# Opening of a two-layer encoder trunk: interleaved first products, token-order squares, and small matmuls at both ends

## The chip, the cores and the metric

The kernel runs on one core of one Trainium2 chip. Time is device microseconds of that core for one execution; the figure compared is the median of the runs of a kernel.

## The reference

One inference step of an encoder for two request groups, one prompt of 512 frames and eight running streams of 16 frames, 640 token columns together, each of 1024 channels, in float32. There are two layers. Each layer computes

- `x += 1/2 * SwiGLU(RMSNorm(x) * g1)` with 2816 hidden columns,
- a mixer: one projection of the norm, a short causal convolution, attention in a band of 64-frame chunks, two gates and an output product,
- a second half step of SwiGLU.

A final RMSNorm ends it. The part that matters here is the very first step and the very last one:

```python
def _rmsnorm(x, g):
    xf = x.astype(jnp.float32)
    y = xf * lax.rsqrt(jnp.mean(xf * xf, axis=-1, keepdims=True) + EPS)
    return y.astype(x.dtype) * g

def _swiglu(h, w_gu, w_down):
    gu = h @ w_gu
    g, u = jnp.split(gu, 2, axis=-1)
    return (jax.nn.silu(g) * u) @ w_down
```

## The kernel before

**Layout.** Channels lie on partitions: x is eight tiles `x[k]` of 128 channels by 640 tokens (SEQ + streams). [...] Weights come as a stream `wst` of slabs of 128 by 1024 (512 KB), each eight blocks of 128 by 128, through three buffers named `raw` (`load`, L245).

**Precision.** Every float32 product is made of three matmuls in a faster float32 format: each operand is split in a high part and a low part (what the high part leaves), and high x high, high x low and low x high are added up in PSUM (`multiply`, L372). So each slab is split too: ScalarE casts it to `whi` (L305), VectorE subtracts to get `wlo` (L310). `prep(i)` casts slab i and leaves its subtraction pending, `flush()` issues what is pending, `source(i)` loads a slab (and for later slabs adds pieces of it), `quiet()` takes the next prepared slab without preparing another. Three buffers each of `whi` and `wlo` exist.

**Seven products.** Most of the feed-forward layers use a scheme in which a 2 by 2 block product takes seven products instead of eight; its seven operands per pair of rows of x are `ex.ops[kp]`, tiles of 7 by 320 columns (high and low). They are made by `Expand.final` from the even row (`E`, three pieces) and the odd row (`O`, five pieces) of a pair.

**The opening** (`opening`, L606 on) does the first four gate and up columns of the first feed-forward layer as eight plain products of 8 rows x 3 x 2 = 48 matmuls, while the operands of the scheme are made beside them for what follows. The norm's factor `rho` is not known at the start, so the products are made of `x * g` alone, and `rho` is multiplied in afterwards. In the kernel before, product 0 follows the rows of x as they come in, then product 1; then ScalarE squares the eight rows of x (L571, L574), VectorE adds them up (L249), PE sums over partitions with a column of ones (`npsa`, L472), ScalarE takes the root (L585), VectorE the reciprocal and a diagonal (L589, L482), and PE spreads it over partitions with `ones` (`nbca`, L595) in row 1 of product 3. The operands of the scheme are made between products 2 and 6 by `final` (L521 to L556). A product writes `po`, one of two double-bank buffers of PSUM; `out(i)` takes it away, and product i + 2 needs that buffer.

**The order of work.** In this stage the orders of PE, VectorE and ScalarE are those in which the code is written (`manual_schedule`); each engine does its list strictly in that order and waits where an input is not there. From the sixth hidden column on only PE's order is written and a planner orders VectorE and ScalarE. Loads of x, weights and tokens are issued by SyncE's queue (SP), in order. In the opening the rows of x and quarters of slab 0 are issued alternately (L415, L421), with slabs 1 and up behind them.

**The end** (`Final.all`): the last down product is made in two parts of columns, 384 and 256 (`PARTS`). After each row of the second part its squares go into `npsf` by matmuls with a column of ones (L1939); then come a root (L1944), reciprocal, diagonal, and one matmul `nbcf` that spreads the result (L1954), and VectorE scales the eight rows and sends them out (L1958, L1960).

Of the kernel before, what the change touches and what calls it, by code (L numbers as in the profile page):

```python
# [10 lines left out]
F32 = mybir.dt.float32  # L11
# [5 lines left out]
P = 128  # L17
# [160 lines left out]


@with_exitstack  # L180
def trunk(ctx: ExitStack, tc: tile.TileContext, xin, wst, small, pbias, samplebias, kcache, vcache,
          yout, ko, vo, co):
    nc = tc.nc
    PE, DVE, ACT, POOL, SP = nc.tensor, nc.vector, nc.scalar, nc.gpsimd, nc.sync
# [123 lines left out]
    def flush():  # L308
        for lo, src, hi in pending:
            DVE.tensor_tensor(out=lo, in0=src, in1=hi.bitcast(F32), op=ALU.subtract)  # L310
        pending.clear()
# [102 lines left out]
    for k in range(KT):  # L414
        SP.dma_start(x[k], xin[:, k, :])  # L415

        if k == 0:
            raws.append(wp.tile([P, CH], F32, tag="raw", name="raw0", bufs=3))
        if k % 2 == 0:
            c = slice(k * P, (k + 2) * P)  # L420
            SP.dma_start(raws[0][:, c], wst[0][:, c])  # L421

    def norm(pool, name, goff, ssum):

# [64 lines left out]
    class Expand(Stats):  # L489
# [10 lines left out]
            self.sq = self.rest = None  # L500
            self.known = False

        def final(self, m, square=True):

            kp, odd = divmod(m, 2)
            n = f"{self.name}_{kp}"
            if not odd:

                self.E = self.fp.tile([P, 3, HT], F32, name=f"xe{n}", tag="even", bufs=1)
                hi = self.fp.tile([P, 7, HT], F32R, name=f"xhi{n}", tag=f"xhi{kp}")  # L510
                lo = self.fp.tile([P, 7, HT], F32R, name=f"xlo{n}", tag=f"xlo{kp}")
                self.ops.append((hi, lo))
            else:

                O = self.fp.tile([P, 5, HT], F32, name=f"xo{n}", tag="odd", bufs=1)
            E = self.E
            hi, lo = self.ops[kp]
            end = m == KT - 1
            g = sm[:, self.goff + m : self.goff + m + 1]
            B = O[:, 3:5] if odd else E[:, 0:3:2]  # L520
            ACT.activation(B, halves(x[m]), AF.Copy, scale=g)  # L521
            if square and end:
                self.sq = tmp(f"sq{self.name}_{m}")
            elif square:
                self.square(m)
            if not odd:
                DVE.tensor_tensor(out=E[:, 1], in0=E[:, 0], in1=E[:, 2], op=ALU.subtract)
                self.flush()
                ACT.copy(hi[:, 5:7], E[:, 0:2])
                self.late.append((lo[:, 5:7], E[:, 0:2], hi[:, 5:7]))  # L530
            else:
                self.flush()
                ACT.copy(hi[:, 3:5], O[:, 3:5])
# [3 lines left out]
                DVE.tensor_tensor(out=O[:, XT7], in0=O[:, 4], in1=E[:, 2], op=ALU.subtract)  # L537
                self.late.append((lo[:, 3:5], O[:, 3:5], hi[:, 3:5]))
                self.flush()

                def rest():
                    ACT.copy(hi[:, 0:3], O[:, 0:3])
# [5 lines left out]
                if not end:  # L548
# [53 lines left out]
    def opening(fp, name, goff, n, put, tails):  # L602

        ACT.copy(early, epst)  # L606
        ex = Expand(fp, name, goff)
        h = []
        whi, wlo = (wp.tile([P, CH], F32R, tag=f"w{t}", name=f"w{t}0", bufs=3) for t in ("hi", "lo"))
        ready.append((whi, wlo))  # L610
        for k in range(KT):
            g = sm[:, goff + k : goff + k + 1]
            hi = hp.tile([P, T], F32R, tag="hhi", name=f"hhi{name}_{k}")
            lo = hp.tile([P, T], F32R, tag="hlo", name=f"hlo{name}_{k}")
            ACT.activation(hi, x[k], AF.Copy, scale=g)
            c = slice(k * P, (k + 2) * P)
            if k % 2 == 0:
                ACT.copy(whi[:, c], raws[0][:, c])
            DVE.scalar_tensor_tensor(out=lo, in0=x[k], scalar=g, in1=hi.bitcast(F32),
                                     op0=ALU.mult, op1=ALU.subtract)  # L620
            if k % 2 == 0:
                DVE.tensor_tensor(out=wlo[:, c], in0=raws[0][:, c], in1=whi[:, c].bitcast(F32),
                                  op=ALU.subtract)
            h.append((hi, lo))
        flush()

        made = {2: (0, 1), 3: (2, 3), 4: (4,), 5: (5, 6), 6: (7,)}
        us, gs, ps = [], [], []

        def out(i):  # L630

            j, up = divmod(i, 2)
            if not up:
                gs.append(tmp(f"g{name}_{j}"))
                if j:
                    scaled(gs[j], ps[i], ex.rho)
                    ACT.activation(gs[j], gs[j], AF.Silu)
                else:
                    ACT.copy(halves(gs[j]), two(ps[i]))
# [9 lines left out]
        def begun():  # L649
            ex.total(att(f"nps{name}"))  # L650
            ex.root()
            ex.diagonal()

        at = {2: {4: begun}, 3: {1: lambda: ex.spread([att(f"nbc{name}_{a}")[:, :HT] for a in range(2)])}}
        for i in range(2 * n):
            ps.append(acc(f"po{name}_{i}"))
            product(ps[i], h, at.get(i, {}))
            if i > 1:
                out(i - 1)
            if i == 0:  # L660
                for k in range(KT):
                    ex.square(k)
                    ex.add()
                    if k == 1:
                        out(0)
                    if k == 4:
                        flush()
            if i == 1:
                continue
            if i == 3:  # L670
                g, u = gs[0], us[0]
                DVE.tensor_tensor(out=g, in0=g, in1=ex.rho, op=ALU.mult)
                ACT.activation(g, g, AF.Silu)
                DVE.tensor_tensor(out=u, in0=u, in1=ex.rho, op=ALU.mult)
            flush()
            for m in made.get(i, ()):
                ex.final(m, False)
            if i == 3:
                DVE.tensor_tensor(out=u, in0=u, in1=g, op=ALU.mult)
            if i == max(made):  # L680
                ex.rest()
        ahead()
        begin()
        out(2 * n - 1)

        def parts(j, u):
            hi = hp.tile([P, T], F32R, tag="hhi", name=f"ahi{name}_{j}")
            lo = hp.tile([P, T], F32R, tag="hlo", name=f"alo{name}_{j}")
            split(hi, lo, u)
            put(j, (hi, lo))  # L690


        for j in sorted(range(n), key=lambda j: j < 2):
            tails.append(lambda j=j: parts(j, us[j]))
        ex.rest = None
        return ex
# [1171 lines left out]
    class Final:  # L1868
# [8 lines left out]
        def all(self, ops):  # L1877
# [9 lines left out]
            for m in range(KT):  # L1887
# [173 lines left out]
def _layout(inputs):  # L2061
# [21 lines left out]
    return {"xin": xin, "wst": _stream(i), "small": small, "pbias": pbias, "samplebias": sbias, "kcache": kc, "vcache": vc}  # L2083


_OUTS = {
# [39 lines left out]
```

## Time and profile before

| | us |
|---|---|
| median of 3 runs | 2496.21 (2496.2 to 2496.61) |
| the profiled execution | 2496.66 |
| its span, first to last instruction | 2494.7 |
| PE busy / weight loads busy | 2478.1 / 2419.0 |
| VectorE busy | 2119.2 |
| ScalarE busy | 1450.0 |
| mean granted clock of TensorE | 0.998 |

In the profile, PE is TensorE's matmuls, PEld its weight loads, DVE VectorE, ACT ScalarE, POOL GpSimd, SP SyncE; L with a number is a line of the kernel; `out<-in` names the tile written and those read. A row in order of time has the start, the busy time, the instruction, how many were merged (x2), and in brackets the idle time before it with what ended it. Matmuls overlap, so the distance between starts tells more than the busy time. A float32 matmul that is not split appears as two passes, each with a weight load of its own.

### The profile page before, as it was taken

The page shows a single profiled execution, that of the slowest core. Times are in us where ns is not written, and L with a number is a line of the kernel's source. Part 1 is how long each engine was busy: PE and PEld are TensorE (multiplying, and loading weights), DVE is VectorE, ACT ScalarE, POOL GpSimd, SP SyncE. Part 2 cuts the span into 40 slices and gives each one's busy share as a digit, 9 for nine tenths or more (in the row PEclk, how much of TensorE's full clock was granted, in tenths as well). Part 3 has the DMA queues.
Part 4 walks back from the last instruction along what each step waited for, and adds up shares of the span by engine and source line. Part 5 has one row for each costly group of instructions (what it writes and reads, how often), then busy time and mean ns, then how long its engine had stood idle before and what let it go on. Part 6 is the DMA issues. An engine that isn't in the chain of part 4 may idle for free.

```text
span 2494.7 us, 43515 instructions
## 1 busy us (share of the span) xinstructions
PE 2478.1 (99%) x17048; PEld 2419.0 (97%) x17048; DVE 2119.2 (85%) x3322; ACT 1450.0 (58%) x2343; POOL 370.7 (15%) x445
## 2 busy tenths in 40 slices
PE   9999999999999999999999999999999999999998
PEld 8999999888999999999999999998899999999998
DVE  7888888878888899888798889888788888989887
ACT  7455556674666555555565555556646665555554
POOL 0011211211111011111001111221111110111111
PEclk9999999999999999999999999999999999999999
DMA  4245665335345344655435555643344553455554
GB/s 146 82 107 124 138 135 130 106 115 167 99 119 145 101 116 118 138 135 135 117 90 126 129 134 123 138 119 115 125 153 104 126 141 95 119 133 122 129 135 110
DMA packets 133261, 308.10 MB, mean 124 GB/s; under 512 B 12768, under 2 KB 76128, under 8 KB 133056
## 3 DMA queue, kind: packets, MB, share of 16 engines
q1 hardware_dynamic: 68976, 219.18, 27.3%
q0 software_dynamic: 63360, 85.50, 20.6%
q8 instruction: 133, 2.18, 0.4%
q10 hardware_dynamic: 720, 0.65, 0.1%
q14 instruction: 72, 0.59, 0.1%
HBM read 221.13 MB, written 7.94 MB: 92 GB/s over the span
## 4 chain that ended last, share of the span: by engine, by line
PE 94%; DVE 3%; ACT 2%; DMA 1%; issue 0%; SPq 0%; DVEq 0%; ACTq 0%
PE pab L395 12%; PE paa L395 11%; PE pcb L395 6%; PE pca L395 6%; PE daa L962 5%; PE dab L962 5%; PE po L372 4%; PE qa L395 4%; PE pbb L395 3%; PE pba L395 3%; PE dca L962 3%; PE dcb L962 3%; PE pda L372 2%; PE pv L1622 2%; PE ma_cv L395 2%; PE qc L395 2%
## 5 line engine op out<-in xcount | busy, mean ns | idle before, releaser
L310 DVE TENSOR_TENSOR wlo<-raw,whi 128x512 fp32r<-128x512 f32 (+1 forms) x583 | 598.6, 1030 | 236.1 <-ACT whi L305 230.6
L305 ACT CAST whi<-raw 128x512 fp32r<-128x512 f32 (+1 forms) x583 | 519.9, 897 | 348.0 <-PE pbb L395 44.6
L305 ACT CAST whi<-s 128x1024 fp32r<-128x1024 f32 (+1 forms) x164 | 153.6, 937 | 248.1 <-issue 107.8
L395 PE MATMUL pab<-xhib,whi 128*128 128x320 f32 x704 | 218.3, 310 | 0.4 <-DVE gb L249 0.4
L395 PE MATMUL pab<-xhib,wlo 128*128 128x320 f32 x704 | 217.4, 309 | 0.0
L395 PE MATMUL pab<-xlob,whi 128*128 128x320 f32 x704 | 217.4, 309 | 0.0
L395 PE MATMUL paa<-xhia,whi 128*128 128x320 f32 x640 | 198.0, 309 | 0.2 <-DVE ga L249 0.2
L395 PE MATMUL paa<-xloa,whi 128*128 128x320 f32 x640 | 197.6, 309 | 0.0
L395 PE MATMUL paa<-xhia,wlo 128*128 128x320 f32 x640 | 197.6, 309 | 0.0
L310 DVE TENSOR_TENSOR wlo<-s,whi 128x1024 fp32r<-128x1024 f32 (+1 forms) x164 | 176.6, 1077 | 10.4 <-ACT whi L305 10.4
L395 PEld LDWEIGHTS pab<-xhib,whi 128*128 128x128 f32 x704 | 132.2, 188 | 1.1 <-DVE gb L249 0.9
L395 PEld LDWEIGHTS pab<-xlob,whi 128*128 128x128 f32 x704 | 132.2, 188 | 0.2
L395 PEld LDWEIGHTS pab<-xhib,wlo 128*128 128x128 f32 x704 | 132.2, 188 | 0.0
L395 PEld LDWEIGHTS paa<-xhia,whi 128*128 128x128 f32 x640 | 120.2, 188 | 0.5 <-DVE ga L249 0.5
L395 PEld LDWEIGHTS paa<-xloa,whi 128*128 128x128 f32 x640 | 120.2, 188 | 0.1
L395 PEld LDWEIGHTS paa<-xhia,wlo 128*128 128x128 f32 x640 | 120.2, 188 | 0.0
L249 DVE TENSOR_TENSOR raw<-raw,raw 128x512 f32<-128x512 f32 x164 | 112.2, 684 | 1.8 <-DMA raw<-in_wst 0.2
L249 DVE TENSOR_TENSOR raw<-s,raw 128x512 f32<-128x512 f32 x164 | 112.3, 685 | 0.0
L395 PE MATMUL pcb<-xhib,whi 128*128 128x320 f32 x352 | 108.7, 309 | 0.0
L395 PE MATMUL pcb<-xlob,whi 128*128 128x320 f32 x352 | 108.7, 309 | 0.0
L395 PE MATMUL pcb<-xhib,wlo 128*128 128x320 f32 x352 | 108.7, 309 | 0.0
L986 POOL DMA_DIRECT2D x<-c_b x52 | 62.6, 1203 | 309.5 <-ACT c_b L979 134.5
(816 smaller groups left out, 8170.8 us busy)
## 6 DMA issues: line engine op xcount, KB each, us to landing
raw<-in_wst SPq DMA_DIRECT2D x375, 512.0 KB, 3.7
x<-c_b POOLq DMA_DIRECT2D x52, 320.0 KB, 5.1
x<-c_a POOLq DMA_DIRECT2D x50, 320.0 KB, 5.0
kc<-in_kcache SPq DMA_DIRECT2D x32, 256.0 KB, 4.1
vc<-in_vcache SPq DMA_DIRECT2D x16, 512.0 KB, 4.5
ub<-cbb POOLq DMA_DIRECT2D x42, 160.0 KB, 5.9
ua<-cba POOLq DMA_DIRECT2D x38, 160.0 KB, 5.4
x<-u_a POOLq DMA_DIRECT2D x18, 320.0 KB, 5.1
```

Source lines behind the costliest of these rows:

```text
L249: DVE.tensor_tensor(out=out, in0=a, in1=b, op=ALU.add)
L305: ACT.copy(hi[:, d], src[:, c])
L310: DVE.tensor_tensor(out=lo, in0=src, in1=hi.bitcast(F32), op=ALU.subtract)
L372: PE.matmul(ps[a] if isinstance(ps, list) else ps[:, a, :HT], w, x[:, a * HT : (a + 1) * HT], start=first and j == 0, stop=last and j == 2)
L395: PE.matmul(ps, a, b, start=start and kp == 0 and j == 0, stop=stop and kp == NP - 1 and j == 2, skip_group_check=True)
L962: PE.matmul(ps[u], w, y, start=start and i == 0 and j == 0, stop=i == 1 and j == 2, skip_group_check=True)
L986: POOL.dma_start(rows(r, cols), z, accum_op=ALU.add)
L1622: PE.matmul(pv[t], xx[:, t * P : (t + 1) * P], w[:, kk * AW : (kk + 1) * AW], start=c == 0 and kk == 0 and j == 0, stop=c == KT // 2 - 1 a ...
```

## The change

1. **Rows interleaved.** Products 0 and 1 run together: each row of x is multiplied into both before the next row (the last two rows together). For that, slab 1 is loaded and split in quarters like slab 0, alternating with the rows of x. For row 0, VectorE instead of ScalarE makes the two high weight parts.
2. **Odd rows kept.** The split of an odd row of x is written into its place among the operands of the scheme (pieces 3 and 4 of `ex.ops`), so that it is not made again. `Expand.final` is no longer called here; its steps are written out as `scale`, `mix`, `high`, `low`.
3. **Token squares.** The input has a second copy of x in token order (`xtok`, five tiles of 128 tokens by 1024 channels). It is loaded by nine transfers behind slab 2 and squared and summed along its rows, tokens 0, 2 and 4 on VectorE, 1 and 3 on ScalarE (all but the first in two halves). The ten npsa passes and the eight squares of rows with their seven additions go.
4. **Orders written out.** What ScalarE and VectorE do between the products is one written list, with the casts of slabs, the copies of products and the operands of the scheme in fixed places. The spread stands at row 3 of product 3 instead of row 1.
5. **Small matmuls.** `stir` issues matmuls of ones with ones that nothing reads: 15 at the start of the opening, 3 and 5 near the end, around the last sum of squares.

```diff
+    def stir(ps, n):
+        for _ in range(n):
+            PE.matmul(ps[:, :P], ones, ones, start=True, stop=True)
...
         if k == 0:
-            raws.append(wp.tile([P, CH], F32, tag="raw", name="raw0", bufs=3))
+            for n in range(2):
+                raws.append(wp.tile([P, CH], F32, tag="raw", name=f"raw{n}", bufs=3))
         if k % 2 == 0:
             c = slice(k * P, (k + 2) * P)
-            SP.dma_start(raws[0][:, c], wst[0][:, c])
+            for n in range(2):
+                SP.dma_start(raws[n][:, c], wst[n][:, c])
...
         ACT.copy(early, epst)
+        stir(att(f"stir{name}"), 15)
         ex = Expand(fp, name, goff)
+        ex.ps = fp.tile([P, NT], F32, name=f"sums{name}", bufs=1)
+        load(2)
+        z = fp.tile([P, D], F32, tag="s65", name=f"tok{name}_0", bufs=1)
+        toks = [[(z, ex.ps[:, 0:1])]]
+        rest = fp.tile([P, NT], F32, name=f"rest{name}", bufs=1)[:, 1:]
+        SP.dma_start(z, xtok[0])
+        for c in range(1, NT):
+            toks.append([])
+            for a, (tag, z) in enumerate((("hhi", ex.ps[:, c : c + 1]), ("hlo", rest[:, c - 1 : c]))):
+                t = hp.tile([P, T], F32, tag=tag, name=f"tok{name}_{c}{a}")[:, : D // 2]
+                toks[c].append((t, z))
+                SP.dma_start(t, xtok[c][:, a * D // 2 : (a + 1) * D // 2])
...
+            if odd:
+                hi, lo = (z[:, 3:5].rearrange("p a b -> p (a b)") for z in ex.ops[kp])
...
             ACT.activation(hi, x[k], AF.Copy, scale=g)
             c = slice(k * P, (k + 2) * P)
-            if k % 2 == 0:
-                ACT.copy(whi[:, c], raws[0][:, c])
+            if not odd:
+                for (whi, _), raw in zip(ready, raws):
+                    (ACT.copy if k else DVE.tensor_copy)(whi[:, c], raw[:, c])
             DVE.scalar_tensor_tensor(out=lo, in0=x[k], scalar=g, in1=hi.bitcast(F32),
                                      op0=ALU.mult, op1=ALU.subtract)
...
-        at = {2: {4: begun}, 3: {1: lambda: ex.spread([att(f"nbc{name}_{a}")[:, :HT] for a in range(2)])}}
...
+        def square(c):
+            for z, total in toks[c]:
+                if c % 2 == 0:
+                    DVE.tensor_tensor_reduce(out=z, in0=z, in1=z, scale=1.0, scalar=0.0, op0=ALU.mult, op1=ALU.add,
+                                             accum_out=total)
+                else:
+                    ACT.activation(z, z, AF.Square, accum_out=total)
...
+        for ks in (*((k,) for k in range(KT - 2)), (KT - 2, KT - 1)):
+            for p, w in zip(ps, ws):
+                for k in ks:
+                    multiply(p, tuple(z[:, k * P : (k + 1) * P] for z in w), h[k], k == 0, k == KT - 1)
+        prep(2)
+        flush()
+        scale(0)
+        mix(0)
+        scale(1)
+        out(0)
+        high(0)
+        square(0)
+        low(0)
+        square(1)
+        out(1)
+        mix(1)
+        high(1)
+        for c in range(2, NT):
+            square(c)
+        prep(3)
+        add(ex.ps[:, 1:], ex.ps[:, 1:], rest)
+        ex.root()
+        flush()
+        ex.diagonal()
+        prep(4)
+        scale(2)
+        mix(2)
+        low(1)
+        high(2)
+        flush()
+        scale(3)
+        plain(2)
+        plain(3, {3: lambda: ex.spread([att(f"nbc{name}_{a}")[:, :HT] for a in range(2)])})
+        out(2)
...
+        for i, m in ((4, 4), (5, 6)):
+            plain(i)
...
+            prep(i + 2)
+            out(i)
+            low(m + 1)
             flush()
...
                 if m == 5:
                     self.ps = acc("npsf1")[:, :, 0]
+                    self.idle = acc("stirf")[:, 0]
...
+            stir(self.idle, 3)
             self.add(self.sq, False, True)
+            stir(self.idle, 5)
             self.root(1)
```

More of the change, by code (lines that the diff above doesn't have):

```diff
@@ L180, in trunk @@
 @with_exitstack
[L181 removed]
+def trunk(ctx: ExitStack, tc: tile.TileContext, xin, xtok, wst, small, pbias, samplebias, kcache, vcache,
           yout, ko, vo, co):
@@ L501, in __init__, with place, final @@
             self.known = False
-        def final(self, m, square=True):
+        def place(self, kp):
+            self.ops.append(tuple(self.fp.tile([P, 7, HT], F32R, name=f"x{t}{self.name}_{kp}", tag=f"x{t}{kp}")
+                                  for t in ("hi", "lo")))
+        def final(self, m, whole=True, hold=False):
+            square = whole
             kp, odd = divmod(m, 2)
@@ L532, in final @@
                 self.flush()
-                ACT.copy(hi[:, 3:5], O[:, 3:5])
+                if whole:
+                    ACT.copy(hi[:, 3:5], O[:, 3:5])
                 for o, a, b in ((XN6, E[:, 1], O[:, 4]), (XT4, O[:, XN6], O[:, 3])):
@@ L547, in final @@
                 self.rest = rest
-                if not end:
+                if not (end or hold):
                     rest()
@@ L608, in opening @@
         h = []
[L609 to L610 removed]
+        for n_ in range(2):
+            ready.append(tuple(wp.tile([P, CH], F32R, tag=f"w{t}", name=f"w{t}{n_}", bufs=3) for t in ("hi", "lo")))
         for k in range(KT):
             g = sm[:, goff + k : goff + k + 1]
[L613 to L614 removed]
+            kp, odd = divmod(k, 2)
+            if odd:
+                hi, lo = (z[:, 3:5].rearrange("p a b -> p (a b)") for z in ex.ops[kp])
+            else:
+                ex.place(kp)
+                hi = hp.tile([P, T], F32R, tag="hhi", name=f"hhi{name}_{k}")
+                lo = hp.tile([P, T], F32R, tag="hlo", name=f"hlo{name}_{k}")
@@ L615, in opening @@
             ACT.activation(hi, x[k], AF.Copy, scale=g)
             c = slice(k * P, (k + 2) * P)
-            if k % 2 == 0:
-                ACT.copy(whi[:, c], raws[0][:, c])
+            if not odd:
+                for (whi, _), raw in zip(ready, raws):
+                    (ACT.copy if k else DVE.tensor_copy)(whi[:, c], raw[:, c])
             DVE.scalar_tensor_tensor(out=lo, in0=x[k], scalar=g, in1=hi.bitcast(F32),
                                      op0=ALU.mult, op1=ALU.subtract)
-            if k % 2 == 0:
-                DVE.tensor_tensor(out=wlo[:, c], in0=raws[0][:, c], in1=whi[:, c].bitcast(F32),
-                                  op=ALU.subtract)
+            if not odd:
+                for (whi, wlo), raw in zip(ready, raws):
+                    DVE.tensor_tensor(out=wlo[:, c], in0=raw[:, c], in1=whi[:, c].bitcast(F32),
+                                      op=ALU.subtract)
@@ new lines, in square, with scale @@
+        def square(c):
[3 more added lines that the diff above has]
+                                             accum_out=total)
+                else:
+                    ACT.activation(z, z, AF.Square, accum_out=total)
+        def scale(m):
+            kp, odd = divmod(m, 2)
+            n_ = f"{name}_{kp}"
+            if odd:
+                ex.O = fp.tile([P, 5, HT], F32, name=f"xo{n_}", tag="odd", bufs=1)
+            else:
+                ex.E = fp.tile([P, 3, HT], F32, name=f"xe{n_}", tag="even", bufs=1)
+            g = sm[:, goff + m : goff + m + 1]
+            ACT.activation(ex.O[:, 3:5] if odd else ex.E[:, 0:3:2], halves(x[m]), AF.Copy, scale=g)
@@ new lines, in mix, with views @@
+        def mix(m):
+            E = ex.E
+            if not m % 2:
+                DVE.tensor_tensor(out=E[:, 1], in0=E[:, 0], in1=E[:, 2], op=ALU.subtract)
+                return
+            O = ex.O
+            for o, a, b in ((XN6, E[:, 1], O[:, 4]), (XT4, O[:, XN6], O[:, 3])):
+                DVE.scalar_tensor_tensor(out=O[:, o], in0=a, scalar=-1.0, in1=b, op0=ALU.mult, op1=ALU.subtract)
+            DVE.tensor_tensor(out=O[:, XT7], in0=O[:, 4], in1=E[:, 2], op=ALU.subtract)
+        def views(m):
+            kp, odd = divmod(m, 2)
+            at, src = (slice(0, 3), ex.O[:, 0:3]) if odd else (slice(5, 7), ex.E[:, 0:2])
+            return src, *(z[:, at] for z in ex.ops[kp])
@@ new lines, in high, with low, plain @@
+        def high(m):
+            src, hi, _ = views(m)
+            ACT.copy(hi, src)
+        def low(m):
+            src, hi, lo = views(m)
+            DVE.tensor_tensor(out=lo, in0=src, in1=hi.bitcast(F32), op=ALU.subtract)
+        def plain(i, at=()):
+            ps.append(acc(f"po{name}_{i}"))
+            pair = quiet()
+            for k in range(KT):
+                if k in at:
+                    at[k]()
+                multiply(ps[i], tuple(z[:, k * P : (k + 1) * P] for z in pair), h[k], k == 0, k == KT - 1)
@@ new lines, in opening @@
+        ps += [acc(f"po{name}_{i}") for i in range(2)]
+        ws = [quiet() for _ in ps]
+        for ks in (*((k,) for k in range(KT - 2)), (KT - 2, KT - 1)):
[12 more added lines that the diff above has]
+        square(1)
@@ new lines, in opening @@
+        DVE.tensor_tensor(out=g, in0=g, in1=ex.rho, op=ALU.mult)
+        ACT.activation(g, g, AF.Silu)
+        DVE.tensor_tensor(out=u, in0=u, in1=ex.rho, op=ALU.mult)
+        low(2)
+        DVE.tensor_tensor(out=u, in0=u, in1=g, op=ALU.mult)
+        mix(3)
+        high(3)
+        prep(5)
+        out(3)
+        low(3)
+        flush()
+        for i, m in ((4, 4), (5, 6)):
+            plain(i)
+            scale(m)
+            mix(m)
+            high(m)
+            low(m)
+            scale(m + 1)
+            mix(m + 1)
+            high(m + 1)
+            prep(i + 2)
+            out(i)
+            low(m + 1)
+            flush()
@@ L682, in opening @@
+        plain(6)
+        prep(8)
+        flush()
+        plain(7)
+        prep(9)
+        out(6)
+        flush()
         ahead()
```

42 lines of the change are left out of this document (6 added, 36 removed).

## The prediction

> **What bounds the kernel now.** I read the page first, then the chain of waits of the matmul engine, then the span in three stretches, and last the two short stretches in order of time. From the page, the waits of PE, and the busy time in three stretches (columns: microseconds, then busy time and count of each engine, granted clock, DMA share, GB/s):
>
> ```profile
> span 2494.7 us, 43515 instructions
> PE 2478.1 (99%) x17048; PEld 2419.0 (97%) x17048; DVE 2119.2 (85%) x3322; ACT 1450.0 (58%) x2343; POOL 370.7 (15%) x445
> ...
> PE poa L372 <- ACT whi L618: 5.6, 1, 5.6
> ...
> 0.00:67.27 67.27, 61.21 (x398) 59.71 (x399) 51.70 (x71) 46.56 (x63) 1.13 (x9) 1.00 0.40 135
> 67.27:2474.90 2407.63, 2405.15 (x16569) 2349.00 (x16568) 2053.71 (x3220) 1397.16 (x2267) 369.52 (x436) 1.00 0.49 123
> 2474.90:2494.70 19.80, 11.74 (x85) 10.30 (x84) 13.83 (x34) 6.27 (x14) 0.00 (x0) 0.81 0.38 132
> ```
>
> TensorE is the bound. It is idle for 16.6 us (2494.7 - 2478.1): 6.06 in the opening, 2.48 in the 2407.63 us between, 8.06 at the end. The change touches only the first and the last stretch. So microseconds are at stake, and time saved in the opening is kept, since nothing between waits for anything but PE. Busy time hides slow matmuls, so I read the opening by starts. PE in order of time (start, busy; a row with x2 is a pair of matmuls):
>
> ```profile
> 5.63 0.90 PE L372 MATMUL poa<-hhia,whi 128*128 128x320 f32 x2 [5.63 <-ACT whi L618]
> ...
> 8.55 0.63 PE L372 MATMUL poa<-hhia,wlo 128*128 128x320 f32 x2
> 9.02 0.46 PE L372 MATMUL poa<-hhia,whi 128*128 128x320 f32 x2
> ...
> 22.84 0.46 PE L372 MATMUL poa<-hhia,whi 128*128 128x320 f32 x2
> ...
> 26.07 0.46 PE L372 MATMUL poa<-hhia,wlo 128*128 128x320 f32 x2
> 26.36 1.17 PE L472 MATMUL npsa<-ones,ssuma 128*128 128x1 f32 x10
> ...
> 27.77 0.45 PE L372 MATMUL poa<-hloa,whi 128*128 128x320 f32 x2
> ...
> 31.58 0.46 PE L372 MATMUL poa<-hhia,wlo 128*128 128x320 f32 x2
> 31.88 1.24 PE L595 MATMUL nbca<-ssuma,ones 128*128 128x320 f32 x4
> ...
> 33.24 0.46 PE L372 MATMUL poa<-hloa,whi 128*128 128x320 f32 x2
> ...
> 66.98 0.46 PE L372 MATMUL poa<-hhia,wlo 128*128 128x320 f32 x2
> 67.27 0.31 PE L395 MATMUL paa<-xhia,whi 128*128 128x320 f32 x1
> ```
>
> From 33.24 to 66.98 there are 115 pairs: 0.2934 us a pair, 0.1467 a matmul, 7.04 for a product of 48. Products 0 and 1 run from 5.63 to 22.84, 17.21 us where 14.08 is the steady price: 3.13 lost. The first 12 matmuls take 3.39 (5.63 to 9.02), 0.28 each, 1.93 times the steady price: 1.63 of the loss is a slow start of the array (the granted clock reads 1.00 there, so that column doesn't show it). The other 1.5 is waits for rows and weights. The ten npsa passes push the next pairs by 27.77 - 26.07 - 2 x 0.2934 = 1.11; nbca by 33.24 - 31.58 - 2 x 0.2934 = 1.07, that is 0.268 a pass of 320 columns, so 0.107 for 128.
>
> **The change part by part.** Rows of the start and of the loads (the raw row: one slice, KB, us from issue to landing):
>
> ```profile
> 0.88 0.21 POOL L404 MEMSET ones<- 128x128 f32 x1
> 1.19 0.41 SPq L421 DMA_DIRECT2D raw<-in_wst  x1
> ...
> 5.19 0.39 ACT L618 CAST whi<-raw 128x256 fp32r<-128x256 f32 x1
> 5.32 0.88 DVE L619 SCALAR_TENSOR_TENSOR hloa<-x,sm,hhia 128x640 fp32r<-128x640 f32 x1 [5.32 <-ACT hhia L615]
> ...
> 6.12 0.42 DVE L622 TENSOR_TENSOR wlo<-raw,whi 128x256 fp32r<-128x256 f32 x1
> ...
> raw<-in_wst SPq DMA_DIRECT2D x1, 128.0 KB, 3.8
> ...
> 4.00:5.00 1.00, 0.00 (x0) 0.00 (x0) 0.00 (x0) 0.54 (x1) 0.26 (x1) 1.00 0.89 300
> 9.00:16.00 7.00, 6.86 (x42) 5.80 (x40) 6.35 (x10) 6.18 (x9) 0.00 (x0) 1.00 1.04 404
> ```
>
> *The 15 small matmuls* need only ones, set at 1.09, so they start near 1.2. Each is two passes (npsa: ten passes for five matmuls), 30 in all. Slow, a pass is 0.107 x 1.93 = 0.206. If the slow time is 3.39 as now, it ends at 4.6: 16.5 slow passes, then 13.5 at 0.107 = 1.45, done at 6.05. All fast would be 4.4, all slow 7.4; I take 6.05, the slow time that the rows show. The array is then fast for the first real matmul: the 1.63 goes.
>
> *First row of the interleaved products.* VectorE now makes both high weight parts ahead of the low part of x. The first slice lands at 1.19 + 3.8 = 5.0, the second 131 KB later at 300 GB/s, 5.45. VectorE: whi0 to 5.4, whi1 to 5.85, low x 0.88 to 6.75, wlo0 7.15, wlo1 7.55. PE: high x high at 6.05, then waits for low x to 6.75; the ten other matmuls of the row follow with small waits and end near 8.35. At 1.76 a row (12 x 0.1467) that is a start at 6.6 in effect, 1 us later than the 5.63 of now, but at full speed.
>
> *Rows 2 to 8.* A row of x now feeds 12 matmuls instead of six. ScalarE's 0.83 a row and VectorE's 0.88, plus two pieces of weights a pair on each (0.39, 0.42), are 2.5 us a pair of rows against 3.52 on PE; loads are 917 KB a pair, at 404 GB/s 2.3. PE is the bound here and the waits go. Products 0 and 1 end at 6.6 + 14.08 = 20.7, instead of 22.84: -2.15.
>
> *The ten npsa passes* are gone from PE: -1.11. Their sums come from squares of rows in token order, with these prices (ScalarE and VectorE in order of time; removed squares and adds first):
>
> ```profile
> 18.00 3.29 ACT L574 ACTIVATE sqa<-x 128x640 f32<-128x640 f32 x5
> 18.76 2.68 DVE L249 TENSOR_TENSOR ssuma<-ssuma,sqa 128x640 f32<-128x640 f32 x3 [0.39 <-ACT sqa L574]
> ...
> 17.43 0.67 ACT L639 COPY ga<-poa 128x640 f32<-128x640 f32 x1
> 22.13 1.98 ACT L305 CAST whi<-raw 128x1024 fp32r<-128x1024 f32 x2
> 25.09 1.22 DVE L310 TENSOR_TENSOR wlo<-raw,whi 128x1024 fp32r<-128x1024 f32 x1
> 30.59 0.73 ACT L529 CAST xhia<-xea 128x640 fp32r<-128x640 f32 x1 [1.44 <-DVE xea L527]
> 33.55 1.00 ACT L542 CAST xhia<-xoa 128x960 fp32r<-128x960 f32 x1 [0.74 <-DVE xoa L537]
> ...
> 496.14 0.71 ACT L1828 ACTIVATE s<-s,st 128x512 f32<-128x512 f32 x1
> 496.76 0.18 ACT L1828 ACTIVATION_READ_ACCUMULATOR s<-s,st 128x1 f32 x1
> ```
>
> ScalarE loses eight squares (0.66 each) and gains four halves at 0.8; VectorE loses seven adds (0.89) and gains one whole and four halves, which I price like ScalarE's. It also loses four casts and four subtractions of odd rows, whose high and low parts the first products already hold. Both engines have less to do; what counts is the order. ScalarE now stands at the copy of product 0 until that ends (20.7 - 1.76 = 18.95), with the following behind it: copy 0.67, high 0.73, two halves 1.6, copy 0.67, high 1.0, two halves 1.6, cast of slab 3 at 1.0: 7.3, so 26.2, and VectorE's low part 1.22 more, 27.5. Product 3 starts at 27.7 and reads that low part 0.59 later, at 28.3. Cover 0.8 us; I cost it at nothing, and every microsecond beyond 0.8 is one on PE. The root, a table load and the diagonal end by about 30; spread stands at row 3 of product 3, 27.7 + 2.64 = 30.4: near, cost nothing. Slabs 4 to 7 are cast one product ahead and have over 1 us.
>
> *The loads.* Nine loads of tokens (2.6 MB) go on SP's queue between slab 2 and slab 3. By slab 3 the queue has moved 7.3 MB (eight rows of 0.33, three slabs and slab 3 of 0.52, tokens): some 0.9 MB by 5 us, at 300 GB/s, the rest at 404, so it lands near 20.9. ScalarE wants it at 25.2: hidden by 4.3. The tokens land before it and before their squares.
>
> *Sum of the opening:* products 2 to 7 and nbca keep their price, 42.24 + 1.07, so the next stage starts at 64.0 instead of 67.27: -3.3. From below: a start at 5.6 with no stall gives 63.0, -4.3. From above: the small matmuls all slow (+1.6, below) and slab 3 a microsecond beyond its cover, -0.7.
>
> **The end.** PE and VectorE in order of time, and one stretch with its granted clock:
>
> ```profile
> 2485.69 0.61 PE L1939 MATMUL npsf<-ones,sqf 128*128 128x1 f32 x4 [0.78 <-ACT sqf L1933]
> ...
> 2487.17 1.14 DVE L1958 SCALAR_TENSOR_TENSOR x<-x,sm,frr 128x384 f32<-128x384 f32 x2
> 2487.31 1.22 PE L1954 MATMUL nbcf<-fsum,ones 128*128 128x256 f32 x2 [1.02 <-DVE fsum L482]
> 2488.57 3.22 DVE L1958 SCALAR_TENSOR_TENSOR x<-x,sm,nbcf 128x256 f32<-128x256 f32 x8 [0.25 <-PE nbcf L1954]
> ...
> 2487.00:2488.00 1.00, 0.69 (x2) 0.50 (x2) 1.00 (x3) 0.00 (x0) 0.00 (x0) 0.50 1.03 366
> ```
>
> Three small matmuls (6 x 0.107 = 0.64) lie in the 0.78 wait ahead of npsf; five (1.07) after it end near 2487.4, about when nbcf may start. With the clock kept at 1.00, two passes of 256 cost 0.43 instead of 0.85. But VectorE is at the previous rows until 2488.3 and only idles 0.25 for nbcf, so the gain is 0.2, not 0.4. Their bank of PSUM is one that nothing in this stage uses, so no copy is waited for. If the clock falls anyway, the five take 2.06 and nbcf starts 1 us late: +1.0.
>
> Sum: -3.3 - 0.2 = -3.5. The profiled execution took 2496.66, 0.45 above the median 2496.21 of the three runs; 2493.16 for it, 2492.7 for the median, 0.14% less. About 0.2%, 5 us, is what a measurement of this kernel can tell from no change, so the forecast is "faster, but within that".
>
> **The rivals.**
> *The warm-up is longer than the small matmuls cover* (A). If the array becomes fast only at 9.02 as now, all 30 passes are slow, end at 7.4, and 1.64 us of real matmuls are still slow (loss 0.79): a start of 8.2 in effect instead of 6.6, total -1.9, 2494.3. For it: nothing in the rows says whether time since the first matmul or a fixed grid decides. Against: three runs within 0.41. [...]
>
> *Slab 3 late* (B), the way to slower: its load stands behind nine token loads. They start behind slab 2, at 13.2. If these and slab 3 move at 140 GB/s, not 404, slab 3 lands at 13.2 + 3.1 MB/140 = 35.3, 10.1 late: 9.3 on PE, -3.5 + 9.3 = +5.8, 2502.0. It decides against the change from 4.3 late (0.8 cover, 3.5 gain). For it: no row has so many loads in a row while ScalarE and VectorE stand in a fixed order. Against: 404 GB/s over 7 us just before.
>
> *The small matmuls at the end run slow* (C): -3.3 + 1.0, 2493.9.
>
> *It does not do what it says* (D): the waits move from products 0 and 1 to 3 and 4 because the fixed order is too tight: about 2496. For it: the cover of 0.8 at slab 3. Against: less work on both engines.
>
> **How the numbers follow.** Forecast 0.6 (own range 2491.9 to 2493.7); A 0.14, C 0.08, D 0.08, B 0.06; 0.04 for a gain beyond my lower bound (-4.3 - 0.25, 2491.7). The range takes forecast, A and C and part of D: 2491.6 to 2495.4. Faster by over 0.2% (under 2491.2) 0.05; slower by over 0.2% (over 2501.2) 0.05; within 0.9.
>
> **What the changed profile would show.** Right: 30 passes on PE from about 1.2 to about 6; first real matmul pairs 0.29 apart; products 0 and 1 ending near 20.7; no npsa; the first paa near 64.0; nbcf's clock at 1.00. Wrong: a wait of PE for wlo or ssum in products 3 to 7; real matmuls 0.53 a pair after the small ones; a wait of ScalarE for raw; more than 2.5 us of idle PE between the opening and the last 20 us.

## The result, and the profile after

The changed kernel takes 2492.76 us (median of 22 runs, 2492.03 to 2493.58); the kernel before, measured beside it, 2496.62 (22 runs, 2495.9 to 2498.74). The ratio is 0.9985, 95% interval 0.9979 to 0.9991: 3.86 us or 0.15% less, a small gain, but one that is clear of the noise. The profiled execution took 2492.73.

The page, and the longest of the waits of PE (what it waited for: us in all, times, longest):

```profile
span 2490.9 us, 43594 instructions
PE 2481.3 (100%) x17084; PEld 2424.0 (97%) x17084; DVE 2115.8 (85%) x3327; ACT 1443.3 (58%) x2340; POOL 370.3 (15%) x445
```

```profile
PE stira L411 <- POOL ones L404: 1.1, 1, 1.1
```

The wait of 5.6 us for the first weights is gone; what heads the list now is the wait for the tile of ones. PE is busy for 3.2 us *more* than before, and the kernel is faster: busy time now counts small matmuls that nothing reads. Only starts tell the gain. The span in three stretches, cut at the first `paa` and at the last group of `npsf`, first the kernel before (its first stretch, 0.00:67.27, stands in the prediction), then the changed one:

```profile
67.27:2485.69 2418.42, 2415.07 (x16647) 2358.28 (x16645) 2061.72 (x3240) 1403.18 (x2279) 369.52 (x436) 1.00 0.49 123
2485.69:2494.70 9.01, 1.82 (x6) 1.01 (x6) 5.82 (x14) 0.26 (x1) 0.00 (x0) 0.57 0.72 247
```

```profile
0.00:64.75 64.75, 63.61 (x419) 63.30 (x419) 48.97 (x77) 40.44 (x61) 1.14 (x9) 1.00 0.50 181
64.75:2482.42 2417.67, 2415.36 (x16653) 2358.77 (x16651) 2061.07 (x3237) 1402.56 (x2279) 369.16 (x436) 1.00 0.47 123
2482.42:2490.90 8.48, 2.32 (x16) 1.92 (x16) 5.72 (x14) 0.26 (x1) 0.00 (x0) 0.85 0.76 264
```

The span is shorter by 3.8 us: 2.52 in the opening, 0.75 in the middle, 0.53 at the end. PE of the opening in order of time:

```profile
1.14 6.36 PE L411 MATMUL stira<-ones 128*128 128x128 f32 x30 [1.14 <-POOL ones L404]
7.26 0.54 PE L372 MATMUL poa<-hhia,whi 128*128 128x320 f32 x2
7.63 0.46 PE L372 MATMUL poa<-hloa,whi 128*128 128x320 f32 x2
7.93 0.46 PE L372 MATMUL poa<-hhia,wlo 128*128 128x320 f32 x2
...
21.42 0.46 PE L372 MATMUL poa<-hhia,whi 128*128 128x320 f32 x2
...
28.46 0.46 PE L372 MATMUL poa<-hhia,whi 128*128 128x320 f32 x2
...
31.11 1.24 PE L608 MATMUL nbca<-ssuma,ones 128*128 128x320 f32 x4
...
64.75 0.31 PE L395 MATMUL paa<-xhia,whi 128*128 128x320 f32 x1
```

A row of x is 640 columns, two matmuls of 320 (x2). The small matmuls last until 7.26; the first real matmuls are fast at once (0.30 us a pair at 7.63). Products 0 and 1 end at 21.42, 14.16 us after their start, against 14.08 for 96 matmuls at the steady price: PE waits for no row in them. From there to `paa` it is 43.33 us, where it was 67.27 - 22.84 = 44.43; the difference is the price of the ten `npsa` passes.

The instructions on which the fixed order hangs, VectorE and then ScalarE in order of time:

```profile
23.29 0.68 DVE L683 CUSTOM_DVE_ANT_0 toka<-toka 128x512 f32<-128x512 f32 x1
...
26.61 1.23 DVE L310 TENSOR_TENSOR wlo<-raw,whi 128x1024 fp32r<-128x1024 f32 x1 [0.52 <-ACT whi L305]
...
28.51 0.83 DVE L488 TENSOR_TENSOR ssuma<-ident,ninva 128x640 f32<-128x640 f32 x1
```

```profile
16.24 1.05 ACT L305 CAST whi<-raw 128x1024 fp32r<-128x1024 f32 x1 [1.00 <-DMA raw<-in_wst]
...
21.08 0.63 ACT L686 ACTIVATE toka<-toka 128x512 f32<-128x512 f32 x1
...
25.54 1.03 ACT L305 CAST whi<-raw 128x1024 fp32r<-128x1024 f32 x1
```

Slab 3's low part is done at 27.84 and its first reader is at 28.46 + 0.59 = 29.05, a cover of 1.2 us; the diagonal is done at 29.34 and is spread at 31.11. In this execution no cast of a whole slab waits for its load except slab 2's, at 16.24, which is not late for PE. Slab 3's load is issued at 18.16 and lands 5.9 us later, at 24.1, 1.5 us before its cast. The end, PE and VectorE together, and one stretch with its granted clock (the last number but two):

```profile
2481.50 0.91 PE L411 MATMUL stirf<-ones 128*128 128x128 f32 x6
2482.42 0.61 PE L2057 MATMUL npsf<-ones,sqf 128*128 128x1 f32 x4
2482.89 1.36 PE L411 MATMUL stirf<-ones 128*128 128x128 f32 x10
...
2484.08 0.66 PE L2072 MATMUL nbcf<-fsum,ones 128*128 128x256 f32 x2
2484.96 3.22 DVE L2076 SCALAR_TENSOR_TENSOR x<-x,sm,nbcf 128x256 f32<-128x256 f32 x8
...
2484.00:2485.00 1.00, 0.74 (x5) 0.34 (x3) 1.00 (x3) 0.00 (x0) 0.00 (x0) 1.00 0.91 327
```

`nbcf` takes 0.66 at a clock of 1.00, where it took 1.22 at 0.50. VectorE's last eight rows begin 2.54 us after the last `npsf` group (before: 2488.57 - 2485.69 = 2.88).

### The profile page after: what moved, and what is told of

Read it like the earlier page. It is cut to its first block, busy times and chain, and to the rows that moved or that the text cites. A ratio compares the mean times of both kernels' runs of the same rounds, so it can differ in the third digit from the quotient of the medians.

```text
span 2490.9 us, 43594 instructions
## 1 busy us (share of the span) xinstructions
PE 2481.3 (100%) x17084; PEld 2424.0 (97%) x17084; DVE 2115.8 (85%) x3327; ACT 1443.3 (58%) x2340; POOL 370.3 (15%) x445
## 4 chain that ended last, share of the span: by engine, by line
PE 95%; DVE 3%; ACT 2%; issue 0%; DVEq 0%; POOL 0%; ACTq 0%; POOLq 0%
PE pab L395 12%; PE paa L395 11%; PE pcb L395 6%; PE pca L395 6%; PE daa L1077 5%; PE dab L1077 5%; PE po L372 4%; PE qa L395 4%; PE pbb L395 3%; PE pba L395 3%; PE dcb L1077 3%; PE dca L1077 3%; PE poa L372 2%; PE pda L372 2%; PE pv L1737 2%; PE ma_cv L395 2%
## 5 line engine op out<-in xcount | busy, mean ns | idle before, releaser
L310 DVE TENSOR_TENSOR wlo<-raw,whi 128x1024 fp32r<-128x1024 f32 (+1 forms) x582 | 597.7, 1030 | 236.1 <-ACT whi L305 230.7
L305 ACT CAST whi<-raw 128x1024 fp32r<-128x1024 f32 (+1 forms) x582 | 518.7, 896 | 350.0 <-PE pbb L395 44.3
```

Source lines behind the costliest of these rows:

```text
L305: ACT.copy(hi[:, d], src[:, c])
```

## The experiments

Two readings of the gain had to be told apart. **S**, the sum: the gain is made of separate terms on PE's path, namely the waits for rows that the interleaving takes away, the ten passes, and the slow start of the array. **W**, the warm-up: the small matmuls at the start make most of it, and the rest of the change is hidden or undone elsewhere. Each edit below undoes or adds one part. Medians are of 11 runs; "the changed kernel" is its 2492.76, taken on an occasion of its own, where the kernel before had 2496.62. The kernel before had 2496.69 beside four of the variants (no small matmuls at the start, none at the end, products in turn, passes back), 2496.82 beside four (15 in the kernel before, three copies, 30, the first 12) and 2496.55 beside the last three (15 again, 12 again, 9). So the occasions differ by some tenths of a microsecond. Two parts of the change, the odd rows kept and the written order, were not undone by themselves.

**No small matmuls at the start.**

```diff
-        stir(att(f"stir{name}"), 15)
+        att(f"stir{name}")
```

> The changed kernel without the 15 small matmuls at the start. Theory S (sum of small terms: waits for rows, npsa passes, slow start): the first real matmul comes near 5.9 us, where VectorE's first parts are ready, and runs slow for 3.3 us or more; if the array gets fast at 9.2, 12 matmuls are done by then instead of 22 and products 0 and 1 end at 21.5; if at 12.6, 24 are done and they end at 23.2. Against 21.42 that is +0.1 to +1.8, middle +0.9 us. Theory W (the warm-up is most of the gain): at least +2.5 us, the whole gain of the opening.

Measured: 2494.18 (2493.41 to 2495.0), 1.4 more than the changed kernel. PE of its opening:

```profile
5.89 0.90 PE L372 MATMUL poa<-hhia,whi 128*128 128x320 f32 x2 [5.89 <-ACT hhia L646]
...
10.22 0.71 PE L372 MATMUL poa<-xloa,whi 128*128 128x320 f32 x2
10.75 0.47 PE L372 MATMUL poa<-xhia,wlo 128*128 128x320 f32 x2
...
65.83 0.31 PE L395 MATMUL paa<-xhia,whi 128*128 128x320 f32 x1
```

Real matmuls go 0.53 us a pair until 10.75, for 4.9 us (3.4 in the kernel before). The opening ends 1.08 later, and 1.62 later than in a second execution of the changed kernel (64.21, below). The small matmuls are worth about a third of the gain, within S's +0.1 to +1.8. The later of S's two cases, an array fast only at 12.6, was an assumption of mine and no run shows it: the longest slow time in the traces, 6.15 us (below), would put it at 12.0.

**Products 0 and 1 one after the other**, all else as in the change.

```diff
-        for ks in (*((k,) for k in range(KT - 2)), (KT - 2, KT - 1)):
+        for ks in (range(KT),):
```

> The changed kernel with products 0 and 1 one after the other, all else the same. Theory S: product 0 then follows the rows; the low part of row 7 is ready at 16.2, so it ends at 16.8 and product 1 at 23.8 instead of 21.42: +2.4 us, with waits of PE for hlo or xlo in product 0. Theory W: the array is fast either way, so +0 to +0.3.

Measured: 2496.64 (2495.71 to 2497.71), 3.9 more: the whole gain is gone. Its waits of PE, then PE in order of time:

```profile
PE poa L372 <- DVE xloa L651: 1.3, 4, 0.4
PE poa L372 <- ACT xhia L646: 1.0, 1, 1.0
```

```profile
16.73 0.56 PE L372 MATMUL poa<-xloa,whi 128*128 128x320 f32 x2 [0.31 <-DVE xloa L651]
...
67.78 0.31 PE L395 MATMUL paa<-xhia,whi 128*128 128x320 f32 x1
```

A row now gives PE six matmuls at a time, 0.88 us of work, and rows come more slowly than that until row 7, at 16.7 (the low parts of rows 3, 5 and 7 are read at 11.99, 14.40 and 16.73, some 1.2 us a row). With the small matmuls in place and the `npsa` passes away, the opening is still 3.0 us longer than in the changed kernel, and 3.6 longer than in its second execution (64.21), whose small matmuls ended as early (6.03, here 6.09). I had expected 2.4; the loss is larger, probably since slab 1's loads and casts, now alternating with the rows, delay the rows of product 0 without serving it (no run takes them apart). So this is the price of the order within the changed kernel, not what interleaving alone would gain in the kernel before. It is against W.

**The kernel before, with the 15 small matmuls only.**

```diff
+        warm = att(f"stir{name}")
+        for _ in range(15):
+            PE.matmul(warm[:, :P], ones, ones, start=True, stop=True)
```

> The kernel before with only the 15 small matmuls put in front. Theory S: product 0 of that kernel waits for its rows (row 7's low part is ready at 14.4 whatever the array does), so its end at 15.1 and all after it stay: -0.2 to +0.4 us. Theory W: -1.5 us or more, the slow start's price of 1.6 or so is gained.

Measured: 2495.9 (2495.31 to 2497.76) against 2496.82 for the kernel before beside it; ratio 0.9998, interval 0.9989 to 1.0007, no difference shown by the interval. PE of its opening:

```profile
1.14 6.00 PE L609 MATMUL stira<-ones 128*128 128x128 f32 x30 [1.14 <-POOL ones L404]
6.90 0.53 PE L372 MATMUL poa<-hhia,whi 128*128 128x320 f32 x2
...
10.44 0.56 PE L372 MATMUL poa<-hloa,whi 128*128 128x320 f32 x2 [0.36 <-DVE hloa L622]
...
16.36 0.56 PE L372 MATMUL poa<-hhia,wlo 128*128 128x320 f32 x2 [0.40 <-DVE wlo L310]
...
67.35 0.31 PE L395 MATMUL paa<-xhia,whi 128*128 128x320 f32 x1
```

The wait at 16.36 stands in the kernel before too:

```profile
16.29 0.56 PE L372 MATMUL poa<-hhia,wlo 128*128 128x320 f32 x2 [0.40 <-DVE wlo L310]
```

The array is fast from the first real matmul, at 6.90, and `paa` starts at 67.35, where it was 67.27. A fast PE only meets the rows and slab 1 sooner and waits for them. The opening thus gains nothing from the warm-up by itself in the execution shown, and has its 1.1 to 1.6 us only where the rows are interleaved: against W. By times alone the case is weaker: the median is 0.9 lower, between S's -0.2 to +0.4 and W's -1.5, and the interval holds both none and 1.5.

**The `npsa` passes back**: five matmuls of one column (ten passes) at row 4 of product 2, their result read by nothing.

```diff
+        def back():
+            z = att(f"back{name}")
+            for c in range(NT):
+                PE.matmul(z[:, c : c + 1], ones, ones[:, 0:1], start=True, stop=True)
-        plain(2)
+        plain(2, {4: back})
```

> The changed kernel with five one-column matmuls (ten passes), read by nothing, put into product 2 at the row where npsa stood. Theory S: +1.1 us, the price of the passes in the trace of before. Rival (they lay beside other work): 0.

Measured: 2494.66 (2493.16 to 2496.77), 1.9 more. One wait of PE, what stands behind it on VectorE, and the end of the opening:

```profile
PE qa L395 <- ACT g L1449: 2.1, 1, 2.1
```

```profile
752.31 0.69 DVE L249 TENSOR_TENSOR raw<-raw,raw 128x512 f32<-128x512 f32 x1 [2.02 <-DMA raw<-in_wst]
...
65.39 0.31 PE L395 MATMUL paa<-xhia,whi 128*128 128x320 f32 x1
```

The opening is 0.64 longer although its small matmuls ended 0.48 sooner than in the changed kernel (6.78 against 7.26): 1.1 for the passes, as the rows of before had it. Most of the rest of this execution's excess is a wait of 2.1 us near 755 us, behind a weight load that took 5.5 us from issue to landing, where three other executions have 3.2 to 3.8. The code there is the same. But the runs of this variant are spread more widely than the others', and whether the edit has a part in that isn't shown: of the median's 1.9, the trace accounts for 1.1.

**Three more copies on ScalarE ahead of slab 3's cast**, of a tile that nothing reads any more.

```diff
+        for _ in range(3):
+            ACT.copy(toks[0][0][0], toks[0][0][0])
         prep(3)
```

> The changed kernel with three copies of 128 by 1024 in place (0.95 us each, 2.85 in all) put on ScalarE ahead of the cast of slab 3; nothing reads them. In the trace of the changed kernel wlo of slab 3 ends at 27.8 and is wanted at 29.05: cover 1.2 us; the spread has 1.8. Theory S (PE is bound by the written orders only beyond their cover): PE waits for wlo of slab 3 and loses 1.4 to 1.9 us. Rival (the opening has several us of cover): 0.

Measured: 2495.64 (2495.23 to 2496.1), 2.9 more. PE of its opening:

```profile
28.93 0.56 PE L372 MATMUL poa<-hhia,whi 128*128 128x320 f32 x2 [1.11 <-ACT whi L305]
...
30.19 0.57 PE L372 MATMUL poa<-hhia,wlo 128*128 128x320 f32 x2 [0.41 <-DVE wlo L310]
...
66.00 0.31 PE L395 MATMUL paa<-xhia,whi 128*128 128x320 f32 x1
```

From the last pair ahead of the first wait, at 27.36, to `paa` it is 38.64 us; in the second execution of the changed kernel (below) the same stretch, 27.63 to 64.21, is 36.58. So 2.85 us of copies cost 2.06, a little more than S's 1.4 to 1.9: slab 3's cast is the next thing behind PE, with about a microsecond to spare, and what goes beyond that is lost. In this execution another 1.0 us went between the start of VectorE's last rows and the end of the span, against the changed kernel's first; the rest of the median's 2.9 isn't accounted for.

**No small matmuls at the end.**

```diff
-            stir(self.idle, 3)
             self.add(self.sq, False, True)
-            stir(self.idle, 5)
```

> The changed kernel without the eight small matmuls at the end. Theory S: the granted clock is 0.50 again when nbcf runs, VectorE idles about 0.25 before the last eight rows, +0.2 to +0.4 us. Rival: the copy into idle time gives nothing, 0.

Measured: 2492.98 (2492.44 to 2494.39), 0.2 more, inside the spread: not told from nothing. Its waits of PE and one stretch:

```profile
PE nbcf L2070 <- DVE fsum L488: 1.0, 1, 1.0
PE npsf L2055 <- ACT sqf L2049: 0.8, 1, 0.8
```

```profile
2485.00:2486.00 1.00, 0.30 (x2) 0.00 (x0) 1.00 (x4) 0.00 (x0) 0.00 (x0) 0.68 0.50 180
```

Both waits of the kernel before are back, but here the clock fell at about 2485.4, when `nbcf` was done, and not ahead of it. The same holds for the kernel before with 15 small matmuls at the start only:

```profile
2486.91 0.70 PE L1957 MATMUL nbcf<-fsum,ones 128*128 128x256 f32 x2 [1.01 <-DVE fsum L482]
```

In both, VectorE's last rows begin 2.54 us after the last `npsf` group, as in the changed kernel. Without the small matmuls the slow `nbcf` comes in some executions (one of these three) and not in others, so the 0.34 us at the end may belong to the one execution of the kernel before that was profiled.

**How many small matmuls**: 30, 12 (twice) and 9 instead of 15, and the changed kernel once more.

```diff
-        stir(att(f"stir{name}"), 15)
+        stir(att(f"stir{name}"), 30)
```

> The changed kernel with 30 small matmuls at the start, twice as many. Theory S: they stand ahead of the first real matmul, which has its inputs by then; 30 more passes at 0.108 are +3.2 us, the whole change but 0.7 us gone, and the real matmuls are fast from the first. Theory W: 0 to +0.5.

> The changed kernel with 12 small matmuls at the start instead of 15. In the traces so far the array gets fast at 3.3 to 5.8 us after the first small matmul, a slow pass takes 0.213 and a fast one 0.108. Theory S: 24 passes end between 4.9 and 6.3, about when the low part of the first row is ready (6.7 in the trace of the changed kernel), 30 end between 5.7 and 7.3; so -0.2 to -0.6 us, most where the array gets fast late. Theory W: +0.3 or more, since three fewer warm it up.

> The changed kernel itself, on the same chip as the two beside it: 2492.8 as its 22 runs gave, 3.9 below the kernel before. It is the measure for the next two.

> 12 small matmuls at the start, now beside the changed kernel on one chip. In one trace its opening was 0.56 us shorter, in its median it stood 0.57 us higher than the changed kernel on another occasion. Theory S: -0.2 to -0.6 against e9_changed_again, or a difference too small for these runs. Rival (12 leave the array slow for longer in most runs, since PE stands idle between the small matmuls and the low part of the first row): +0.3 to +0.6.

> Nine small matmuls at the start: 18 passes, at 0.213 done at 5.0, so PE stands idle for 0.8 us before the first real matmul. [...]

| small matmuls | median, us | lowest to highest | first real matmul | `paa` |
|---|---|---|---|---|
| 30 | 2496.2 | 2495.12 to 2497.16 | 9.23 | 66.71 |
| 15, first time | 2492.76 | 2492.03 to 2493.58 | 7.26 | 64.75 |
| 15, again | 2493.22 | 2492.73 to 2493.78 | 6.03 | 64.21 |
| 12 | 2493.33 | 2492.35 to 2494.36 | 6.28 | 64.19 |
| 12, again | 2492.52 | 2491.99 to 2493.19 | 6.11 | 64.19 |
| 9 | 2492.95 | 2492.17 to 2495.24 | 5.79 | 64.11 |

With 30, PE of the opening:

```profile
1.14 8.33 PE L411 MATMUL stira<-ones 128*128 128x128 f32 x60 [1.14 <-POOL ones L404]
9.23 0.53 PE L372 MATMUL poa<-hhia,whi 128*128 128x320 f32 x2
```

The median is 3.4 higher, as S said (+3.2): what goes beyond the first row's arrival costs its full time. The changed kernel again, PE and then ScalarE's cast of slab 3:

```profile
1.14 5.14 PE L411 MATMUL stira<-ones 128*128 128x128 f32 x30 [1.14 <-POOL ones L404]
6.03 0.53 PE L372 MATMUL poa<-hhia,whi 128*128 128x320 f32 x2
...
6.95 0.56 PE L372 MATMUL poa<-hloa,whi 128*128 128x320 f32 x2 [0.39 <-DVE hloa L651]
```

```profile
25.91 1.05 ACT L305 CAST whi<-raw 128x1024 fp32r<-128x1024 f32 x1 [0.81 <-DMA raw<-in_wst]
```

The same 30 passes took 6.1 us in the first of these executions and 4.9 in this one. Where the small matmuls end early, as here, with 12 (both times) and with 9, the second pair starts at 6.7 to 7.0 and `paa` comes at 64.1 to 64.2 whatever the count: the low part of row 0 then sets the start.

The traces also record from when the full clock was granted: from 8.93 us in the kernel before, 6.93 in the first of these two executions, 4.38 in this one, 10.77 without small matmuls. Each agrees with the starts to 0.1 us. The stretch of full clock, up to the fall at the end, lasts 2478.076, 2481.489, 2484.903 or 2488.316 us in the thirteen traces, so these lengths differ by whole steps of 3.413 us. In the eleven executions that start with small matmuls, all at 1.14, the clock rises anywhere from 4.04 to 7.28: the time since the first matmul alone does not decide it.

The first 12 stood 0.57 above the changed kernel, which was measured on another occasion, against S's -0.2 to -0.6, though its opening was 0.56 shorter in the trace. Side by side on one chip, 12 stood 0.70 below 15, the way of S, and 9 stood 0.27 below. Taken from the kernel before beside each, 15 gave 3.86 and 3.33 us, 12 gave 3.49 and 4.03, and 9 gave 3.60, with two of its eleven runs above 2494.9. No run here settles which of these counts is best.

## Why the prediction was right

It forecast 2492.7 within 2491.6 to 2495.4, and a gain of 3.5 us; measured were 2492.76 and 3.86 us. The mechanism held, and the gain, 0.15%, lies within 0.2%, as forecast. That the median fell within 0.1 is luck: the forecast was taken from 2496.21, the median of three runs of the kernel before, where 22 gave 2496.62, and the gain was larger by about as much. For the profiled execution the sum came out through errors that cancel: 0.8 us less than forecast in the opening, 0.75 more in the middle and 0.3 more at the end.

- *Rows 2 to 8, and the waits of products 0 and 1.* Held. In the changed kernel PE waits for no row after the first, and with the rows taken in turn the whole gain goes (+3.9).
- *The npsa passes*, 1.11. Held: 44.43 became 43.33, and putting the passes back costs 1.1 in the opening.
- *The 15 small matmuls.* This is the term that was mis-sized. I took 3.39 us of slow time from the one start that the trace of before shows, hence an end at 6.05, an effective start of 6.6, products 0 and 1 at 20.7 and `paa` at 64.0. In the profiled execution the passes end at 7.26, products 0 and 1 at 21.42, and `paa` comes at 64.75: 0.75 late. In the second execution of the same kernel they end at 6.03, there is the forecast wait of 0.39 for the low part of row 0, and `paa` comes at 64.21, 0.2 from the sum. So the working is right for a slow time near 3 us, and the slow time isn't a constant: a slow pass is 0.213 us, a fast one about 0.11, and by these 30 passes in 6.12 us hold some 27 slow ones (5.8 us), 30 in 4.89 some 15 (3.3 us), 60 in 8.09 some 14 (3.0 us). The start without small matmuls gives 4.9 directly. By the recorded clock it is 2.90 to 6.15 us over the thirteen traces.
- *Rival A* had this length (30 slow passes, an end at 7.4) and was half right in that execution: the length came, but the slow real matmuls that it put behind them did not, because the array was just becoming fast. The slow time differs between executions of one program, 3.24 and 5.79 us in the two of the changed kernel, though the first small matmul starts at 1.14 in both. The 3.39 that I took lies near the short end of what the traces have: four of the thirteen have 2.90 to 3.35.
- *Costed at nothing: slab 3, spread, loads.* PE lost nothing to them in the two executions of the changed kernel, as forecast, but the loads were mis-sized. In the first execution the cover is 1.2 us at slab 3 (forecast 0.8) and 1.8 at the spread, since the token squares were cheaper than I priced them, 0.62 us start to start for a half on either engine, not 0.8. But slab 3 was forecast to land near 20.9, 4.3 us before it is wanted; it landed at 24.1, and in the second execution, issued at 19.98, at 25.9. There its cast waits 0.81 for it, the low part is done at 28.22 with its reader at 28.51, and the cover is 0.3 us, set by the load and not by ScalarE's list. With 9 small matmuls the same wait is 1.05, the cover is 0.05, and PE loses 0.1 at that pair. By the waits of SyncE's queue, the issue at 19.98 stood 1.7 us behind a load of tokens; why that load was slower than in the first execution stays open. So the waits of ScalarE for `raw`, one of the signs of being wrong, came and cost PE nothing; rival B did not come, but its cause was nearer than the working had it, and three copies of delay show the same of D.
- *Costed at nothing: the middle.* Not forecast: 0.75 us less. 0.5 of it is one wait of the kernel before, which the changed kernel's trace lacks:

```profile
PE po L372 <- ACT ya L1435: 0.3, 1, 0.3
```

  Two matmul starts there, at 781 us, lie 0.65 apart instead of 0.15. The code at that place isn't changed. Waits in the gates near 755 us range from none shown to 2.1 us over executions of the variants, whose code there is the same, and the one of 2.1 stands behind a late load; so this looks like variation from one execution to the next. For the wait at 781 itself that is argued, not shown.
- *The end*, -0.2. The clock stayed at 1.00 and `nbcf` was fast, as forecast; the start of VectorE's last rows moved by 0.34, the other 0.2 came in what follows that start, the rows and their stores, which moved by as much as 1.0 us between executions of the variants. Rival C did not come. That the small matmuls there are worth 0.2 could not be separated from nothing.

The gain is thus about 1.4 for the fast array, 1.1 for the passes, and the rest, by subtraction, for the row waits and the end, and these are not independent: the interleaving pays 3.9 when it is taken from the full change, because without it a fast PE waits for rows.

## What to carry to other kernels

Read the distance between the starts of the engine that is the bound, against its steady price (here 0.2934 us a pair), and not its busy time: PE was busy for 3.2 us more in the kernel that is 3.86 us faster. The warming matmuls paid here only up to the arrival of the first real operands and only where the operands behind them came fast enough: alone they did not shorten the opening (`paa` at 67.35, without them at 67.27), and 30 instead of 15 cost 3.4 us. When a term rests on one row of one execution, such as the time until the array is fast, give it the spread of two such rows before taking it to tenths.

## What the runs showed of the hardware

The time from the first matmul to the fast array was 2.90 to 6.15 us over the thirteen traces, and 3.24 and 5.79 in two executions of one program. The granted clock of the views read 1.00 throughout the opening all the same; the starts show the slow time, and so does the recorded start of the full clock. The lengths of the full clock, 2478.076 to 2488.316 us, lie whole steps of 3.413 us apart; with the first matmul at 1.14 each time, the full clock began at 4.04 to 7.28. At the end, with pauses of PE of 0.8 and 1.0 us in each case, the clock fell ahead of `nbcf` in one execution (`nbcf` took 1.22 us at 0.50) and after it in two (0.70). One weight load in the middle of the kernel took 5.5 us to land in one execution and cost PE 2.1 us there; it took 3.2 to 3.8 in three others, where PE waited 0.4 or less.
